# Layer norm's channel sums as two fp32r matmuls on high and low parts, and a last token tile that accumulates on top of sums that ScalarE has laid into PSUM

## The chip, the core and the metric

The kernel runs on one core of one Trainium2 chip. TensorE (PE in the profile; PEld is its weight load), VectorE (DVE), ScalarE (ACT), GpSimd (POOL) and SyncE (SP) run their own instruction streams and wait for one another by semaphores. The metric is the device time of one execution in microseconds; the time before is the median of three runs.

## What is computed

One decoder layer on 1024 tokens of 1024 channels in float32: a Conformer convolution branch and a gated linear recurrence are merged, projected and added to the input; a squared-ReLU MLP follows, and a last RMSNorm. The change touches two places: the layer norm in the convolution branch, and the end, where the MLP's result is added to the residual and normalised.

```python
def layer_norm(x, g, b):
    mu = jnp.mean(xf, axis=-1, keepdims=True)
    xc = xf - mu
    y = xc * lax.rsqrt(jnp.mean(xc * xc, axis=-1, keepdims=True) + EPS)
    return y * g + b
...
u = jax.nn.silu(layer_norm(u, ln_g[l], ln_b[l]))       # after the width-31 convolution
y_a = jnp.einsum("bsc,cd->bsd", u, w_a_out[l])
...
f = jnp.square(jax.nn.relu(jnp.einsum("bsd,df->bsf", h, w_1[l])))
x = x + jnp.einsum("bsf,fd->bsd", f, w_2[l])
return rms_norm(x, g_final)
```

## The kernel before

Every large product is made in float32 precision out of fp32r matmuls. An operand is split into a high part (a ScalarE `Copy` into an fp32r tile) and a low part (the source minus the high part, by VectorE, or by an accumulating DMA that GpSimd issues), and three matmuls are accumulated: high by high, high by low, low by high. A matmul takes 128x128 weights and 512 columns, one PSUM bank of float32. The stages, in the order of time, are the projections from the input with the convolution and the recurrence, the branch products, the output projection, the MLP's first matrix, and its second.

**Layer norm (span 628 to 763 us).** Channels lie along the partitions and tokens along the free axis, so a mean over channels is a product with a 128x128 matrix of 1/1024 (`onesm`, line 110), which also spreads the result over all partitions. The eight channel tiles of the convolution are added up beforehand by accumulating DMAs into one 128x1024 tile `ysum` (`sum_up`, lines 599 to 608). The layer norm runs beside the product of the other branch, `b_mm(j)` for j = 0 to 7 (line 1107): 72 matmuls each, whose two results are gated by `b_out` (line 1123, VectorE at line 1127). `n_mean` (line 1146) is called within `b_mm(2)` and issues one plain float32 matmul for each half of the tokens into banks `mu0` and `mu1`; `n_center` (line 1152) subtracts the mean from the eight pieces of each half (VectorE), squares them (ScalarE) and adds the squares up into `vacc[o]` (VectorE); `n_var` (line 1174), at the start of step j = 4, issues one float32 matmul for each half; `n_root` and `n_scale` (lines 1180 and 1189) make the reciprocal root and apply it. In this stage the order of ScalarE, VectorE, TensorE, SP and GpSimd is that of the program text (`manual_schedule(engines=ENGINES)`, line 1632); `later` puts VectorE work into a list that `vector_work` issues. Tiles come from pools: `T` has 37 buffers of 128x1024 (line 37), the pool behind `EV` has 14 of 128x512 (line 1073), `bank` has 8 PSUM banks.

**The end (span 1496 us to the end).** Seven partial results of the second MLP matrix have been summed into `acc` tiles and two PSUM tiles `keep`; `fold(q2)` (line 1929, VectorE) combines them with the residual into `res`, the sums so far of four token tiles. The last group of channels is multiplied directly: `last_mm(t)` (line 1942) takes 24 matmuls for token tile t, 12 for each half of the output columns, in the order t = 0, 1, 4, 5, then 2, 3, 6, 7. Tiles 0 to 6 of the order use the pool of tags `d`; tile 7 uses two tiles of the pool that held `keep`, one for each half, so that its first half can be read while its second half is being multiplied. `finish(t)` (line 1964) adds `res` to each half (VectorE, line 1973), squares with a running sum (ScalarE, line 1974), makes the reciprocal root in small steps, scales by it and by `gfin`, and stores. For t = 7 the scaling by `gfin` is done ahead (line 1979), and the two halves are scaled (lines 1985 and 1987) and stored from two queues. Here the order on the engines is the compiler's scheduler's: it takes the ready instruction of highest priority, and `finish(7)` has its priority raised by 100 places.

Of the kernel before, what the change touches and what calls it, by code (L numbers as in the profile page):

```python
# [10 lines left out]
F32R = mybir.dt.float32r  # L11
I32 = mybir.dt.int32
AF = mybir.ActivationFunctionType
ALU = mybir.AluOpType

P = 128
S = 1024
D = 1024
HS = 512
# [6 lines left out]
EPS = 1e-6  # L26
# [5 lines left out]
def trunk_kernel(ctx: ExitStack, tc: tile.TileContext, x, xt_in, xt_eo, vecs, w_in, w_a_out, w_b_out,  # L32
                 w_rg, w_o, w_1, w_2, g_final, out):

    nc = tc.nc
    cp = ctx.enter_context(tc.tile_pool(name="consts", bufs=1))
# [8 lines left out]
    def T(name, dt=F32, shape=(P, S)):  # L45
        return tp.tile(list(shape), dt, tag="T", name=name)
# [8 lines left out]
    HALVES = (slice(0, HS), slice(HS, S))  # L55
# [53 lines left out]
    make_identity(nc, ident)  # L109
    onesm = cp.tile([P, P], F32, name="onesm")  # L110
    nc.gpsimd.memset(onesm, 1.0 / D)
    ones = cp.tile([P, P], F32, name="ones")
    nc.gpsimd.memset(ones, 1.0)

# [307 lines left out]
    MM = 0.227  # L422
    TAP = 0.67

    def at(e, cost, ready=0.0):
        clk[e] = max(clk[e], ready) + cost
        return clk[e] + 0.1
# [152 lines left out]
    ysum = []  # L580
# [18 lines left out]
    def sum_up(now, most=8):  # L599

        while summed and summed[0][0] <= now and most:
            most -= 1
            j = summed.pop(0)[1]
            if not ysum:
                ysum.append(T("ysum"))
                nc.gpsimd.dma_start(ysum[0], yd[j])
            else:
                nc.gpsimd.dma_start(ysum[0], yd[j], accum_op=ALU.add)
# [91 lines left out]
    todo, fresh = [], []  # L700

    def later(ready, cost, f, *a):

        todo.append((ready, len(todo), cost, f, a))
# [87 lines left out]
    for i in range(2, NZ):  # L792
        n = zseq.index((i, 1))
# [19 lines left out]
    with tc.manual_schedule(engines=ENGINES):  # L813
        for s in range(3, NC1):
# [49 lines left out]
            for d in range(6):  # L864
                if s - d in EXP:
# [10 lines left out]
                    t = 3 * g + d - 2 - lag  # L876
# [27 lines left out]
    vp = stage.enter_context(tc.tile_pool(name="evac", bufs=7, reuse_waits="tile"))  # L904
# [168 lines left out]
    vp = early.enter_context(tc.tile_pool(name="evac3", bufs=14, reuse_waits="tile"))  # L1073
# [6 lines left out]
    def bank(name):  # L1080
        return zp.tile([P, HS], F32, tag="z", name=name)

    def low(l, src, h):
        tt(l, src, h.bitcast(F32), ALU.subtract)  # L1084
# [58 lines left out]
    def n_pieces(o):  # L1143
        return [(kk, c2, i) for kk in range(2) for c2 in range(2) for i in range(2)]

    def n_mean():
        for o in range(2):
            mean[o] = bank(f"mu{o}")
            nc.tensor.matmul(mean[o], onesm, ysum[0][:, HALVES[o]], start=True, stop=True)
            at("P", 4 * MM)  # L1150

    def n_center(o):
        held = []
# [18 lines left out]
        dve(0.63, held[0][0], add, held[0][1])  # L1172

    def n_var(o):
        pv = bank(f"var{o}")
        nc.tensor.matmul(pv, onesm, vacc[o], start=True, stop=True)
        at("P", 4 * MM)
        rstd[o] = pv

    def n_root(o):  # L1180
        pv = rstd[o]
# [450 lines left out]
    with tc.manual_schedule(engines=ENGINES):  # L1632
        for j in range(8):
            clk["A"], clk["V"] = max(clk["A"], clk["P"] + 0.5), max(clk["V"], clk["P"] - 2)
            if j == 0:
                b_load(1)
                b_gate(0)
            if j == 4:
                n_var(0)
                n_var(1)  # L1640
            if j:
                b_out(j - 1)
            b_gate(j + 1) if j < 7 else None
            b_mm(j)
            if j < 7:
                b_parts(j + 1)
            if j < 6:
                b_load(j + 2)
            vector_work(clk["V"])
            if j < 2:  # L1650
                sum_up(clk["P"])
                vector_work(math.inf if j else clk["P"] - 0.3)
                if j:
                    n_load()
                    sum_up(math.inf)
            elif j < 4:
                n_center(j - 2)
            elif j == 4:
                n_root(0)
                n_root(1)  # L1660
            elif j == 5:
                for b in (0, 1, 3, 2):
                    n_scale(b % 2, b // 2)
            elif j == 6:
                g_parts("a", 1, 0)
                g_parts("a", 1, 1)
                g_load("a", 0, 0)
                g_load("a", 1, 0)
            else:
                g_load("a", 2, 0)  # L1670
                g_get(0, g_lhs)
                g_load("a", 3, 0)
                g_get(1, g_lhs)
                g_t("a", 0, 1, 2)
                g_t("a", 1, 1, 2)
                g_parts("a", 2, 0)
                g_get(2, g_lhs)
                g_parts("a", 2, 1)
                g_load("a", 0, 1)
                g_get(3, g_lhs)  # L1680
                g_load("a", 1, 1)
            vector_work(clk["V"])
        b_out(7)
        for n in range(len(gseq) + 1):
            clk["A"], clk["V"] = max(clk["A"], clk["P"] + 0.5), max(clk["V"], clk["P"] - 2)
            g_get(n - 1, g_post)
            if n in (o0 + 22, u0 + 2):
                x1_root(int(n > u0))
            if n > o0:
                vector_work(clk["V"])  # L1690
                if n == u0:
                    to_mlp()
            g_get(n + 3, g_gate)
            g_get(n, g_mm)
            g_get(n + 4, g_lhs)
            g_get(n + 5, g_sums)
            for f, *a in GX.get(n, ()):
                f(*a)
            vector_work(clk["P"] - 0.3)
# [239 lines left out]
        tt(a[5], a[5], x22[q2], ALU.add)  # L1939
        return (a[2], a[3]), (a[4], a[5])  # L1940

    def last_mm(t):
        r0 = t // 4
        c0 = t % 4 * P
        if t < 7:
            ps = pd.tile([P, S], F32, tag="d", name=f"e{t}", bufs=2)
            outs = [ps[:, h] for h in HALVES]
        else:
            outs = [pk.tile([P, S], F32, tag="k", name=f"e{t}{c}", bufs=2)[:, 0:HS] for c in range(2)]
        for c, o in enumerate(outs):  # L1950
            todo, late = [], []
            for kk in range(2):
                ah, al = (v3(a) for a in last["a", 10 * (r0 + 1) + kk + 1])
                b_h, b_l = (v3(a) for a in last["b", 10 * (kk + 1) + c + 1])
                for k in range(KC):
                    w, wl = ah[:, k, c0:c0 + P], al[:, k, c0:c0 + P]
                    todo += [(w, b_h[:, k, :]), (wl, b_h[:, k, :])]
                    late += [(w, b_l[:, k, :])]
            todo += late
            for n, (a, b) in enumerate(todo):  # L1960
                nc.tensor.matmul(o, a, b, start=n == 0, stop=n == len(todo) - 1)  # L1961
        return outs

    def finish(t, pss, res):
        o = T(f"out{t}")
        y = T(f"y_{t}")
        rows = out.rearrange("(n o) d -> o n d", o=2)[t // 4, (t % 4) * P:(t % 4 + 1) * P, :]
        st = cp.tile([P, 6], F32, tag="stl", name=f"st_last{t}", bufs=2)
        sa, sb, v, s, u, r = (st[:, i:i + 1] for i in range(6))
        lo, hi = HALVES  # L1970
        for hf, a in ((0, sa), (1, sb)):
            h = HALVES[hf]
            tt(y[:, h], res[hf][:, HALVES[t % 2]], pss[hf], ALU.add)
            nc.scalar.activation(o[:, h], y[:, h], AF.Square, accum_out=a)
            if t == 7 and hf == 0:
                nc.vector.tensor_scalar(sa, sa, 1.0 / D, EPS, ALU.mult, ALU.add)
        if t == 7:
            for h in HALVES:
                tt(y[:, h], y[:, h], gfin[:, h], ALU.mult)
            nc.vector.scalar_tensor_tensor(v, sb, 1.0 / D, sa, ALU.mult, ALU.add)  # L1980
            nc.scalar.activation(s, v, AF.Sqrt)
            nc.vector.reciprocal(r, s)
            nc.vector.scalar_tensor_tensor(u, r, v, r, ALU.mult, ALU.mult)
            nc.vector.tensor_scalar(u, u, -0.5, 1.5, ALU.mult, ALU.add)
            nc.vector.tensor_scalar(o[:, lo], y[:, lo], r, u, ALU.mult, ALU.mult)
            nc.sync.dma_start(rows[:, lo], o[:, lo])
            nc.vector.tensor_scalar(o[:, hi], y[:, hi], r, u, ALU.mult, ALU.mult)
            nc.scalar.dma_start(rows[:, hi], o[:, hi])
        else:
            tt(v, sa, sb, ALU.add)  # L1990
            nc.vector.tensor_scalar(v, v, 1.0 / D, EPS, ALU.mult, ALU.add)
            newton_rstd(r, v, s, u)
            nc.vector.scalar_tensor_tensor(o, y, r, gfin, ALU.mult, ALU.mult)
            nc.sync.dma_start(rows, o)

    for q2 in range(2):
        res = fold(q2)
        for t in (2 * q2, 2 * q2 + 1, 4 + 2 * q2, 5 + 2 * q2):
            pss = last_mm(t)
            with tc.high_priority(100 if t == 7 else 0):  # L2000
                finish(t, pss, res[t // 4])

# [83 lines left out]
```

## Time and profile before

| | |
|---|---|
| median of 3 runs | 1550.47 us (1550.38 to 1551.23) |
| the profiled execution, own time | 1550.73 us |
| its span, first to last instruction | 1548.9 us |
| outside the span | 1.83 us |
| granted TensorE clock, mean | 0.998 |
| matmuls | 6804, busy 1537.6 us |
| VectorE, ScalarE, GpSimd busy | 1213.1, 900.4, 189.0 us |

In the rows of a timeline the first number is the start in us from the span's start, the second the time from the start of the first to the end of the last instruction of the row, then the engine, the line, the operation with its output and inputs, the shape and the count; square brackets give idle time of the engine ahead of it and what ended it. Rows of one engine overlap by some hundredths of a microsecond, and matmuls by more, because they are pipelined: what a matmul costs is read from start to start. `sq` is the name in the profile for the tile `vacc[o]` as well, `e` for the last tiles, `st_last` for the small columns of `finish`.

### The profile page before, as it was taken

What the parts mean: (1) busy time and instruction counts of PE and PEld (TensorE: products, weight loads), DVE (VectorE), ACT (ScalarE), POOL (GpSimd) and SP (SyncE); (2) the same over time, 40 slices, a digit from 0 to 9 for tenths busy, and PEclk for the clock granted to TensorE, in tenths of its full rate; (3) what the DMA queues carried; (4) which work ended last, traced back from release to release, by engine and by line L of the source; (5) the groups of instructions that cost most, each with busy time, mean ns of one, the idle gap of its engine ahead of it and who ended that gap; (6) DMA issues with size and microseconds to landing.
All of it is one profiled execution on the core that took longest, in us unless ns stands there. A gap on an engine that the chain in (4) does not pass through costs nothing. (4 is left out here: it accounts for less than half of the span.)

```text
span 1548.9 us, 19074 instructions
## 1 busy us (share of the span) xinstructions
PE 1537.6 (99%) x6804; PEld 1264.6 (82%) x6804; DVE 1213.1 (78%) x1640; ACT 900.4 (58%) x1260; POOL 189.0 (12%) x226
## 2 busy tenths in 40 slices
PE   9999999999999999999999999999999999999997
PEld 7878888788888888878888888888888888888886
DVE  6999989999899983468568869765555558888897
ACT  6748677576667667435275777445444475555552
POOL 0000000002222222000022322000000011111110
PEclk9999999999999999999999999999999999999999
DMA  8653654678999789854579878523333779888852
GB/s 347 169 127 93 162 138 135 156 229 215 263 265 258 194 209 258 275 187 121 184 199 302 197 168 207 207 75 131 114 118 109 238 214 235 225 222 221 197 123 109
DMA packets 124943, 294.18 MB, mean 190 GB/s; under 512 B 12464, under 2 KB 30512, under 8 KB 124848
## 3 DMA queue, kind: packets, MB, share of 16 engines
q1 hardware_dynamic: 93312, 213.00, 40.5%
q0 software_dynamic: 31392, 79.71, 28.1%
q8 instruction: 53, 0.87, 0.2%
q14 instruction: 42, 0.34, 0.1%
q10 hardware_dynamic: 144, 0.26, 0.1%
HBM read 152.93 MB, written 58.72 MB: 137 GB/s over the span
## 5 line engine op out<-in xcount | busy, mean ns | idle before, releaser
L734 PE MATMUL z<-xh,win_h 128*128 128x512 f32 x400 | 124.8, 390 | 0.0
L734 PE MATMUL z<-xl,win_h 128*128 128x512 f32 x400 | 123.4, 389 | 0.0
L1858 DVE TENSOR_TENSOR acc<-acc,d 128x1024 f32<-128x1024 f32 x72 | 87.8, 1219 | 33.4 <-PE d L1846 32.7
L734 PE MATMUL z<-xh,win_l 128*128 128x512 f32 x400 | 99.4, 391 | 0.0
L734 PEld LDWEIGHTS z<-xh,win_l 128*128 128x128 f32 x400 | 75.1, 188 | 16.9
L734 PEld LDWEIGHTS z<-xh,win_h 128*128 128x128 f32 x400 | 75.0, 188 | 16.6 <-ACT win_h L68 0.4
L647 DVE SCALAR_TENSOR_TENSOR y<-u,vec,y 128x511 f32<-128x511 f32 (+14 forms) x120 | 88.3, 736 | 0.0
L734 PEld LDWEIGHTS z<-xl,win_h 128*128 128x128 f32 x400 | 75.1, 188 | 15.8
L647 DVE SCALAR_TENSOR_TENSOR yt<-u,vec,yt 128x511 f32<-128x511 f32 (+6 forms) x112 | 82.5, 736 | 0.0
L647 DVE SCALAR_TENSOR_TENSOR y<-yt,csum,y 128x511 f32<-128x511 f32 (+6 forms) x112 | 82.4, 736 | 0.0
L541 ACT ACTIVATE g<-rg,vec 96x1024 f32<-96x1024 f32 x32 | 35.6, 1114 | 79.6 <-PE rg L531 79.5
L1526 ACT ACTIVATE o<-s 128x512 fp32r<-128x512 f32 x58 | 34.7, 623 | 52.8 <-DVE s L1511 31.3
L67 POOL DMA_DIRECT2D win_l<-win_raw x25 | 21.7, 867 | 319.6 <-ACT win_l L66 259.6
L475 DVE SCALAR_TENSOR_TENSOR v<-xb,vec,v 128x1023 f32<-128x1023 f32 (+2 forms) x36 | 46.2, 1282 | 11.4 <-ACT v L466 10.4
L67 POOL DMA_DIRECT2D zo<-zw x42 | 36.3, 864 | 134.0 <-ACT zo L66 120.6
L1120 PE MATMUL yb<-hgh,wb_h 128*128 128x512 f32 x168 | 52.6, 394 | 0.0
L1120 PE MATMUL yb<-hgl,wb_h 128*128 128x512 f32 x168 | 51.8, 389 | 0.0
L66 ACT ACTIVATE zo<-zw 128x512 fp32r<-128x512 f32 x42 | 26.3, 626 | 30.4 <-DMA zw<-in_w_in_dram 8.4
L67 POOL DMA_DIRECT2D db_1l<-wr x7 | 6.0, 862 | 309.7 <-DMA wr<-in_w_dram 254.0
L1120 PE MATMUL yb<-hgh,wb_l 128*128 128x512 f32 x168 | 41.0, 389 | 0.0
L1084 DVE TENSOR_TENSOR o<-s,o 128x512 fp32r<-128x512 f32 x58 | 38.8, 683 | 0.0
L1120 PEld LDWEIGHTS yb<-hgh,wb_h 128*128 128x128 f32 x168 | 31.6, 188 | 7.4 <-issue 1.0
(1783 smaller groups left out, 4666.7 us busy)
## 6 DMA issues: line engine op xcount, KB each, us to landing
w_raw<-in_w_dram SPq DMA_DIRECT2D x36, 512.0 KB, 5.6
fr<-fd SPq DMA_DIRECT2D x32, 512.0 KB, 5.8
wr<-in_w_dram SPq DMA_DIRECT2D x32, 512.0 KB, 6.5
zw<-in_w_in_dram SPq DMA_DIRECT2D x28, 512.0 KB, 5.8
win_raw<-in_w_in_dram SPq DMA_DIRECT2D x25, 512.0 KB, 4.2
win_l<-win_raw POOLq DMA_DIRECT2D x25, 512.0 KB, 4.5
zo<-zw POOLq DMA_DIRECT2D x42, 256.0 KB, 5.4
gates<-zg SPq DMA_DIRECT2D x32, 256.0 KB, 3.8
```

The costliest lines, as they stand in the source:

```text
L66: nc.scalar.activation(l, src, AF.Copy, scale=-1.0)
L67: nc.gpsimd.dma_start(l, src, accum_op=ALU.add)
L475: nc.vector.scalar_tensor_tensor(v[:, d:S], a[:, 0:S - d], cbw_c[:, w * 12 + t:w * 12 + t + 1], v[:, d:S], ALU.mult, ALU.add)
L541: nc.scalar.activation(a, gps.pop((n, gi))[:HD, :], AF.Sigmoid, bias=(ba_c, bx_c)[gi][:, n:n + 1])
L647: nc.vector.scalar_tensor_tensor(o[:, k:], a[:, 0:HS - k], c, o[:, k:], ALU.mult, add)
L734: nc.tensor.matmul(zps[s][:, HALVES[hf]], w[:, k, :], xw[k][part][hf], start=n == 0, stop=n == 23)
L1084: tt(l, src, h.bitcast(F32), ALU.subtract)
L1120: nc.tensor.matmul(ps[hf], a, b[:, HALVES[hf]], start=n == 0, stop=n == len(todo) - 1)
L1526: nc.scalar.activation(o[:, 0], src, AF.Copy)
L1858: tt(acc[p, q2], acc[p, q2], ps, ALU.add)
```

## The change

1. A constant `onesr` (1/1024 as fp32r, 128x128) is made once by ScalarE.
2. `ysum` is split into two 128x1024 tiles from pool `T`: high by ScalarE, low by VectorE. This new function `n_parts` is called at the end of step j = 1.
3. `n_mean` multiplies each half with two fp32r matmuls (high, then low) instead of one float32 matmul.
4. `n_var` splits `vacc[o]` into two 128x512 tiles from the pool behind `EV` (ScalarE, then VectorE), and multiplies in the same way.
5. For token tile 7, ScalarE copies `res` into the two PSUM tiles ahead of the matmuls, which then accumulate on top. `finish(7)` has no addition any more: ScalarE squares straight from PSUM, and VectorE multiplies PSUM by `gfin` into `y`.

```diff
+    onesr = cp.tile([P, P], F32R, name="onesr")
...
+    def n_sum(name, h, l):
+        ps = bank(name)
+        nc.tensor.matmul(ps, onesr, h, start=True, stop=False)
+        nc.tensor.matmul(ps, onesr, l, start=False, stop=True)
+        at("P", 2 * MM)
+        return ps
+
+    def n_parts():
+        nc.scalar.activation(onesr, onesm, AF.Copy)
+        at("A", 0.3)
+        for n in "hl":
+            ysum.append(T(f"ysum{n}", F32R))
+        nc.scalar.activation(ysum[1], ysum[0], AF.Copy)
+        later(at("A", 1.0), 1.2, low, ysum[2], ysum[0], ysum[1])
+
     def n_mean():
         for o in range(2):
-            mean[o] = bank(f"mu{o}")
-            nc.tensor.matmul(mean[o], onesm, ysum[0][:, HALVES[o]], start=True, stop=True)
-            at("P", 4 * MM)
+            mean[o] = n_sum(f"mu{o}", *(a[:, HALVES[o]] for a in ysum[1:]))
...
     def n_var(o):
-        pv = bank(f"var{o}")
-        nc.tensor.matmul(pv, onesm, vacc[o], start=True, stop=True)
-        at("P", 4 * MM)
-        rstd[o] = pv
+        h, l = (vp.tile([P, HS], F32R, tag="ev", name=f"va{n}{o}") for n in "hl")
+        nc.scalar.activation(h, vacc[o], AF.Copy)
+        low(l, vacc[o], h)
+        rstd[o] = n_sum(f"var{o}", h, l)
...
                 if j:
                     n_load()
                     sum_up(math.inf)
+                    n_parts()
...
-    def last_mm(t):
+    def last_mm(t, res):
...
+            for o, a in zip(outs, res[r0]):
+                nc.scalar.activation(o, a[:, HALVES[t % 2]], AF.Copy)
...
-                nc.tensor.matmul(o, a, b, start=n == 0, stop=n == len(todo) - 1)
+                nc.tensor.matmul(o, a, b, start=n == 0 and t < 7, stop=n == len(todo) - 1,
+                                 skip_group_check=t == 7)
...
         for hf, a in ((0, sa), (1, sb)):
             h = HALVES[hf]
+            if t == 7:
+                nc.scalar.activation(o[:, h], pss[hf], AF.Square, accum_out=a)
+                tt(y[:, h], pss[hf], gfin[:, h], ALU.mult)
+                if hf == 0:
+                    nc.vector.tensor_scalar(sa, sa, 1.0 / D, EPS, ALU.mult, ALU.add)
+                continue
             tt(y[:, h], res[hf][:, HALVES[t % 2]], pss[hf], ALU.add)
             nc.scalar.activation(o[:, h], y[:, h], AF.Square, accum_out=a)
-            if t == 7 and hf == 0:
-                nc.vector.tensor_scalar(sa, sa, 1.0 / D, EPS, ALU.mult, ALU.add)
         if t == 7:
-            for h in HALVES:
-                tt(y[:, h], y[:, h], gfin[:, h], ALU.mult)
             nc.vector.scalar_tensor_tensor(v, sb, 1.0 / D, sa, ALU.mult, ALU.add)
```

More of the change, by code (lines that the diff above doesn't have):

```diff
@@ L1998, in trunk_kernel @@
         for t in (2 * q2, 2 * q2 + 1, 4 + 2 * q2, 5 + 2 * q2):
-            pss = last_mm(t)
+            pss = last_mm(t, res)
             with tc.high_priority(100 if t == 7 else 0):
```

## The prediction, made before the changed kernel was run

> **What bounds the kernel now.** First the page's shares of the engines, then the busy time by stretches of the span, then TensorE's list of waits.
>
> ```profile
> PE 1537.6 (99%) x6804; PEld 1264.6 (82%) x6804; DVE 1213.1 (78%) x1640; ACT 900.4 (58%) x1260; POOL 189.0 (12%) x226
> ```
> ```profile
> 628.00:700.00 72.00, 72.00 (x312) 58.22 (x311) 39.84 (x55) 23.94 (x34) 0.00 (x0) 1.00 0.64 216
> 700.00:760.00 60.00, 60.00 (x267) 49.69 (x266) 37.74 (x46) 24.63 (x34) 0.00 (x0) 1.00 0.41 128
> 1540.00:1548.90 8.90, 0.00 (x0) 0.00 (x0) 3.43 (x9) 0.93 (x3) 0.00 (x0) 0.69 0.32 119
> ```
> ```profile
> PE spare L344 <- POOL ones L113: 1.6, 1, 1.6
> PE gu4a L1283 <- ACT u_late L1337: 0.5, 1, 0.5
> ```
>
> TensorE is busy for 99% of the span. The first two stretches hold the layer norm: in 132 us TensorE is busy for 132 us (the second figure), VectorE for 77.6 and ScalarE for 48.6. So a microsecond of TensorE's work removed there is a microsecond of the end, and work given to VectorE and ScalarE is free while TensorE doesn't wait for it. The last stretch is the other kind: TensorE is done, and a chain of short instructions sets the time. The change touches one thing of each kind.
>
> After its start (`spare`) TensorE waits once, at `gu4a`. Saved time would be lost there if the work it waits for didn't itself go back to TensorE.
>
> ```profile
> 932.43 5.36 DVE L452 SCALAR_TENSOR_TENSOR x<-x,vec,rbm 128x512 f32<-128x512 f32 x8 [1.21 <-PE rbm L1452]
> 939.97 2.36 DVE L452 TENSOR_TENSOR gt2u<-x,x 128x1024 f32<-128x1024 f32 x2
> 943.47 1.05 ACT L1225 ACTIVATE gu6h<-gt2u 128x1024 fp32r<-128x1024 f32 x1
> 958.08 0.58 ACT L1337 ACTIVATE u_late<-gu4a 128x512 f32<-128x512 f32 x1
> ```
>
> It does: VectorE starts at 932.43 on TensorE's `rbm` and then works through to `gt2u`, ScalarE splits that at 943.47 and works nearly without a break to 958.08. All of it moves forward with TensorE.
>
> **The sums over channels.** I take TensorE's starts at the boundaries of the 72-matmul blocks from its timeline.
>
> ```profile
> 661.24 0.62 PE L1120 MATMUL yb<-hgh,wb_h 128*128 128x512 f32 x2
> ...
> 668.50 1.88 PE L1149 MATMUL mu<-ysum,onesm 128*128 128x512 f32 x4
> ```
> ```profile
> 679.33 0.62 PE L1120 MATMUL yb<-hgh,wb_h 128*128 128x512 f32 x2
> ```
> ```profile
> 695.66 1.88 PE L1176 MATMUL var<-sq,onesm 128*128 128x512 f32 x4
> ```
> ```profile
> 713.75 0.61 PE L1120 MATMUL yb<-hgh,wb_h 128*128 128x512 f32 x2
> ```
>
> Block 3 alone lasts from 679.33 to 695.66: 16.33 us, or 0.227 for each of 72 fp32r matmuls. Block 2 with the two means in it lasts 679.33 - 661.24 = 18.09 us, and the two variances with block 4 last 713.75 - 695.66 = 18.09 us. Each pair of float32 sums so costs 1.76 us. Afterwards a pair is four fp32r matmuls of the very form of block 3, 4 x 0.227 = 0.91 us. Each pair gives back 0.85 us, both **1.70 us**.
>
> The Trainium skill (FP8 and Floating Point Precision, TensorE Precision Notes) counts a float32 product as four passes through the array. By that a pair would cost 8 x 0.227 = 1.81 us and the change would give 1.81 us here; the two starts, 18.09 and 16.33, say a little less, and the sum keeps 1.70.
>
> What is added lies beside TensorE's work. For the means:
>
> ```profile
> 594.95 1.22 POOL L608 DMA_DIRECT2D ysum<-yd  x1
> ...
> 656.00 0.85 ACT L1098 ACTIVATE wb_h<-wb_raw 128x768 fp32r<-128x768 f32 x1 [3.22 <-PE yb L1120]
> ...
> 661.21 1.29 DVE L1127 TENSOR_TENSOR sb<-yb,sb 128x512 f32<-128x512 f32 x2 [11.25 <-PE yb L1120]
> ```
>
> The last addition into `ysum` is issued at 594.95, over 50 us ahead. In ScalarE's order the copies `onesr` and `ysumh` come before the row at 656.00, ahead of which it idles 3.22 us; the copy of 128x1024 costs about 1.05 (the `gu6h` row has the form), the small one less. VectorE's low part, about 1.2 by its `gt2u` row (2.36 for two of that size), falls into 11.25 idle microseconds ahead of 661.21. TensorE needs both at 668.50: over 7 us to spare. TensorE has a new wait there, with the rest of block 2 queued behind it; every microsecond of lateness would be paid in full.
>
> For the variances:
>
> ```profile
> 691.00 1.57 ACT L1098 ACTIVATE wb_h<-wb_raw 128x768 fp32r<-128x768 f32 x2
> 691.13 0.69 DVE L1156 TENSOR_TENSOR sq<-sq,sq 128x512 f32<-128x512 f32 x1 [0.16 <-ACT sq L1167]
> ```
>
> The last addition of squares ends at 691.82. Behind it come one ScalarE copy (under 0.8, the cost of one of the larger two at 691.00; the other half's has already run) and one VectorE subtraction (0.69): 693.3 at the latest. TensorE arrives at 695.66 - 0.85 = 694.8, so 1.5 us are left. Queued behind the new copies on ScalarE are the two copies at 691.00, which start up to 1.6 us later; their tiles belong to block 5, which starts at 713.75. This is the thinner cover. Were it gone, block 4 and all behind it would wait.
>
> No DMA is added. Two more tiles of 37, and four of 14, are taken for some microseconds. Who could wait for a buffer is SP with the gates' loads and what is queued behind them:
>
> ```profile
> 686.20 1.77 SPq L1105 DMA_DIRECT2D sb<-gates  x2
> 697.81 1.20 SPq L1091 DMA_DIRECT2D wb_raw<-in_w_b_out_dram  x2
> ```
>
> The gates' load that may be pushed out is the one at 686.20, until the variances have been multiplied at the latest (about 696); the next on SP goes at 697.81 as it is. I take nothing for it.
>
> **The last token tile.** The first two rows are the end of tile 6's matmuls and its first addition; the others are the chain behind TensorE's last matmul.
>
> ```profile
> 1534.00 0.62 PE L1961 MATMUL e<-lb22l,la22h 128*128 128x512 f32 x2
> ...
> 1534.66 1.28 DVE L1973 TENSOR_TENSOR y<-acc,e 128x512 f32<-128x512 f32 x2
> ...
> 1539.22 0.61 PE L1961 MATMUL e<-lb22l,la22h 128*128 128x512 f32 x2
> 1539.85 0.68 DVE L1979 TENSOR_TENSOR y<-y,gfin 128x512 f32<-128x512 f32 x1
> 1540.45 0.68 DVE L1973 TENSOR_TENSOR y<-acc,e 128x512 f32<-128x512 f32 x1
> 1541.16 0.63 ACT L1974 ACTIVATE out<-y 128x512 f32<-128x512 f32 x1 [2.51 <-DVE y L1973]
> 1541.70 0.19 ACT L1974 ACTIVATION_READ_ACCUMULATOR out<-y 128x1 f32 x1
> 1541.92 0.69 DVE L1979 TENSOR_TENSOR y<-y,gfin 128x512 f32<-128x512 f32 x1 [0.79 <-ACT out L1974]
> 1542.53 0.15 DVE L1980 SCALAR_TENSOR_TENSOR st_last<-st_last 128x1 f32<-128x1 f32 x1
> ```
>
> TensorE ends at 1539.83; call it E. The addition starts at E + 0.62, since VectorE is still scaling the first half; the square at E + 1.33; the scaling by `gfin` at E + 2.09, since it overwrites what the square reads; the step that joins the sums at E + 2.70. From there on nothing changes.
>
> Afterwards the square starts as soon as TensorE ends. What the trace doesn't show directly is a square from PSUM with a running sum beside a VectorE read of the same bank in this place, but an earlier stage has just that pair:
>
> ```profile
> 922.84 0.60 ACT L1414 ACTIVATE sq<-tr 128x512 f32<-128x512 f32 x1 [0.48 <-PE tr L1409]
> 923.34 0.19 ACT L1414 ACTIVATION_READ_ACCUMULATOR sq<-tr 128x1 f32 x1
> 923.57 4.87 DVE L1418 COPY x1r<-tr 128x512 f32<-128x512 f32 x8 [3.19 <-ACT sq L1414]
> ```
>
> VectorE had been idle for 3.19 us, TensorE's tile was ready for both, and it waited until ScalarE had read the bank and given out its sum: 0.73 us after the square's start. I take the same order here, because the square stands first in the program. VectorE's wait for TensorE is 0.04 us (tile 6: 1534.66, after matmuls that end at 1534.00 + 0.62). So: square at E + 0.04, product with `gfin` at E + 0.77, and, a step of 0.61 later (1541.92 to 1542.53), the join at E + 1.38. That is **1.32 us** earlier than E + 2.70. The bounds: with no waiting of VectorE at all, the join needs only the square's sum, E + 0.77 and a gain of 1.93; with VectorE held up by tile 6 up to one scaling longer, a gain of 0.1.
>
> Is VectorE free at E + 0.77?
>
> ```profile
> 1537.19 0.20 ACT L98 ACTIVATE st_last<-st_last 128x1 f32<-128x1 f32 x1 [0.42 <-DVE st_last L1991]
> ...
> 1538.58 1.29 DVE L1993 SCALAR_TENSOR_TENSOR out<-y,st_last,gfin 128x1024 f32<-128x1024 f32 x1
> ```
>
> Tile 6's final scaling runs from 1538.58 to 1539.87. If tile 7's first square takes ScalarE ahead of tile 6's root (1537.19), and its first product then takes VectorE, the scaling moves back by some 0.7 us, to end near 1540.55; the product is due at E + 0.77 = 1540.60. Just free.
>
> The copies of `res` into PSUM are new (ScalarE, SBUF to PSUM, a form that this trace lacks). The nearest rows are 0.58 (from PSUM, `u_late`) and 0.63 (within SBUF, line 1974); I take 0.6 each. What counts is when they can run:
>
> ```profile
> 1519.60 1.22 DVE L1937 TENSOR_TENSOR acc<-acc,acc 128x1024 f32<-128x1024 f32 x1
> 1522.20 1.22 DVE L1939 TENSOR_TENSOR acc<-acc,xb 128x1024 f32<-128x1024 f32 x1
> 1525.95 0.63 ACT L1974 ACTIVATE out<-y 128x512 f32<-128x512 f32 x1 [3.43 <-DVE st_last L105]
> ```
>
> The sums are complete at 1520.8 and 1523.4, ScalarE idles 3.43 us ahead of 1525.95, and tile 7's 24 matmuls of 0.227 begin at about E - 5.4 = 1534.4. Ten microseconds of cover, if the scheduler takes them when they are ready, as it does with `fold`'s own additions, which the program has behind tile 5 and VectorE ran between earlier tiles. They cost nothing then.
>
> **Sum.** 1.70 + 1.32 = 3.02 us. The profiled execution would go from 1550.73 to 1547.71, its span from 1548.9 to 1545.9. It lies 0.26 above the median of the three runs, and from that median the forecast is 1550.47 - 3.02 = **1547.45 us**.
>
> **The rivals.**
>
> *The two reads of a bank go side by side.* Then the join comes at E + 0.77 and 0.61 more is gained: 1546.84. Only the shape of the new code speaks for it; the row at 923.57 speaks against it. The Trainium skill (PSUM — Partial Sum Buffer, PSUM bank collisions raise a hardware error) says of ScalarE and VectorE reads too that they must not meet in a bank and have to be guarded by semaphores; the wait of 3.19 us agrees. Chance 0.05.
>
> *Tile 6 is in the way.* If its final scaling starts just ahead of tile 7's second product, VectorE is up to 1.2 us late (1.29 less overlap): 1547.45 + 1.2 = 1548.65 at the most. For it: the margin above is 0.05 us. Against it: tile 6's steps are all ready earlier, and the priority favours tile 7. Chance 0.08.
>
> *ScalarE copies `res` too late: slower than before.* If the copies queue where the program has them, behind tile 6's squares and its root, the first starts at about 1537.4 and ends at 1538.0, where tile 7 would have begun at 1534.4: TensorE waits 3.6 us, 0.6 more than all that is gained, which gives 1551.05. It decides from the point where the first copy starts after 1533.8; the gain is gone when it starts after about 1536.8. For it: the copies stand behind `finish(6)` in the program and have no raised priority. Against it: their inputs are ready ten microseconds earlier, and ScalarE is idle. Chance 0.06.
>
> *The layer norm's gain is lost on the way* to a wait that is not TensorE's own, at `gu4a` or in a load that comes later because its buffer does. Then 1.32 remain: 1549.15. For it: VectorE is busy for 78% of the span, so some stage may stand near its limit. Against it: the one wait listed and its origin in TensorE. Chance 0.06. *Buffers or the scheduler's order change more than that*, with waits beyond what is saved, over 1553.6: chance 0.03.
>
> **How the numbers follow.** The forecast has 0.72. A change of 0.2%, 3.1 us, is about what a measurement of this kernel can tell from none, and the forecast lies at that very bound (1547.37): half of its chance falls on either side, as the scatter of the runs (0.85 us between three) and the few hundredths in the terms decide. Faster by over 0.2%: 0.36 + 0.05, and 0.05 of the two middle rivals, whose terms can turn out smaller, 0.46. Slower by over 0.2%: 0.03. Between: 0.51. The forecast with its terms' bounds is 1546.9 to 1548.0; the range takes in the side-by-side reads and most of tile 6's case and leaves out the late copies and what lies beyond: 1546.6 to 1548.8.
>
> **What would show it.** From block 2's start to block 3's 17.24 us instead of 18.09, and the same for the variances; no wait of TensorE at `mu` or `var`; the copies of `res` in ScalarE's row near 1520 to 1525; the square 0.04 after TensorE's last matmul; the product with `gfin` 0.73 after the square's start and waiting for ScalarE; 1.38 us from TensorE's end to the join, and from there 6.4 us to the span's end as before (1548.9 - 1542.53). A new gap in TensorE's row between 690 and 700 us or after 1533, or a longer wait at `gu4a`, would make the prediction wrong.

## The result, and the profile after

The changed kernel takes 1548.58 us, the median of 22 runs; the kernel before 1551.45 us, also of 22, the first three of which are the runs of the table above. The ratio is 0.9983, with a 95% interval of 0.9976 to 0.9989: **0.17% faster**. The forecast was 1547.45 us. Of the 1.13 us between, 0.98 is the starting point (1551.45 instead of the 1550.47 of three runs); the change itself was forecast at 3.02 us and came out, between the medians, at 2.87.

| | before | after |
|---|---|---|
| profiled execution, own time | 1550.73 us | 1549.04 us |
| its span | 1548.9 us | 1547.2 us |
| TensorE busy | 1537.6 us | 1535.6 us |
| granted TensorE clock, mean | 0.998 | 0.998 |

First, from TensorE's timeline of the kernel after, the layer norm: the start of block 2, matmuls of the means, the start of block 3, the first matmul of the variances, the start of block 5.

```profile
661.46 0.61 PE L1121 MATMUL yb<-hgh,wb_h 128*128 128x512 f32 x2
...
668.72 0.39 PE L1149 MATMUL mu<-ysumh,onesr 128*128 128x512 f32 x1
668.96 0.40 PE L1150 MATMUL mu<-ysuml,onesr 128*128 128x512 f32 x1
...
669.42 0.39 PE L1150 MATMUL mu<-ysuml,onesr 128*128 128x512 f32 x1
...
678.72 0.62 PE L1121 MATMUL yb<-hgh,wb_h 128*128 128x512 f32 x2
...
695.04 0.40 PE L1149 MATMUL var<-vah,onesr 128*128 128x512 f32 x1
...
712.29 0.62 PE L1121 MATMUL yb<-hgh,wb_h 128*128 128x512 f32 x2
```

Block 2 lasts 678.72 - 661.46 = 17.26 us and the variances with block 4 last 712.29 - 695.04 = 17.25, each instead of 18.09: 1.67 us given back. The matmuls of a sum start 0.23 to 0.24 us apart, as fp32r matmuls do in block 3, and no bracket shows idle time ahead of them.

Now the end, from the timeline of all engines: TensorE's last matmuls, tile 6's final scaling, and the chain behind the last matmul.

```profile
1537.83 1.29 DVE L2013 SCALAR_TENSOR_TENSOR out<-y,st_last,gfin 128x1024 f32<-128x1024 f32 x1
1539.00 0.62 PE L1978 MATMUL e<-lb22l,la22h 128*128 128x512 f32 x2
1539.03 0.68 DVE L1993 TENSOR_TENSOR y<-e,gfin 128x512 f32<-128x512 f32 x1
1539.63 0.14 DVE L1995 TENSOR_SCALAR st_last<-st_last 128x1 f32<-128x1 f32 x1
1539.65 0.60 ACT L1992 ACTIVATE out<-e 128x512 f32<-128x512 f32 x1 [1.97 <-PE e L1978]
1540.15 0.19 ACT L1992 ACTIVATION_READ_ACCUMULATOR out<-e 128x1 f32 x1
1540.37 0.69 DVE L1993 TENSOR_TENSOR y<-e,gfin 128x512 f32<-128x512 f32 x1 [0.60 <-ACT out L1992]
1540.98 0.15 DVE L2000 SCALAR_TENSOR_TENSOR st_last<-st_last 128x1 f32<-128x1 f32 x1
```

TensorE ends at E = 1539.62. The square starts at E + 0.03; the product with `gfin` is held by ScalarE (the bracket) until 0.72 after the square's start; the join is at E + 1.36 instead of E + 2.70. That is 1.34 us.

But E itself moved by only 0.21 us, from 1539.83 to 1539.62. TensorE's list of waits after shows the larger part of the reason.

```profile
PE gu4a L1297 <- ACT u_late L1351: 1.6, 1, 1.6
PE z L258 <- ACT xh L227: 0.5, 1, 0.5
PE z4e L933 <- DMA zo<-zs: 0.2, 1, 0.2
PE z L258 <- DVE xl L231: 0.2, 1, 0.2
```

The wait at `gu4a` has grown from 0.5 to 1.6 us, and three short waits in the first stages are new. The balance of the two spans: block 2 starts 0.22 later (first stages), the sums give 1.67, between block 5 and E 1.25 is lost, 1.1 of it at `gu4a`, the end gives 1.34, and the stores behind the join take 6.22 instead of 6.37. Together 0.22 - 1.67 + 1.25 - 1.34 - 0.15 = -1.69 us, the -1.7 of the spans. So in this pair of executions the gain of the sums seems to be lost at `gu4a`, while the medians of many runs show nearly all of it. Which of the two holds had to be tried.

### The profile page after: what moved, and what is told of

It reads as the page before. It is cut to its first block, busy times and chain, and to the rows that moved or that the text cites. A ratio compares the mean times of both kernels' runs of the same rounds, so it can differ in the third digit from the quotient of the medians.

```text
span 1547.2 us, 19086 instructions
## 1 busy us (share of the span) xinstructions
PE 1535.6 (99%) x6804; PEld 1264.6 (82%) x6804; DVE 1214.5 (78%) x1641; ACT 903.6 (58%) x1266; POOL 188.6 (12%) x226
```

## The experiments

The theories. **A:** `gu4a` hangs on a load that lands when it lands; a TensorE that comes 1.67 us earlier waits that much longer there, and the gain of the sums is lost. **B:** the landing of that load scatters from execution to execution, whatever the kernel, so the wait at `gu4a` does too; on the mean the gain passes through. The load can be seen in both kernels, in the timelines of ScalarE and VectorE. Before:

```profile
939.97 2.36 DVE L452 TENSOR_TENSOR gt2u<-x,x 128x1024 f32<-128x1024 f32 x2
942.41 0.63 ACT L66 ACTIVATE gu<-w_raw 128x512 fp32r<-128x512 f32 x1 [3.82 <-DMA w_raw<-in_w_dram]
943.47 1.05 ACT L1225 ACTIVATE gu6h<-gt2u 128x1024 fp32r<-128x1024 f32 x1
```

After:

```profile
938.51 2.35 DVE L453 TENSOR_TENSOR gt2u<-x,x 128x1024 f32<-128x1024 f32 x2
942.07 0.63 ACT L66 ACTIVATE gu<-w_raw 128x512 fp32r<-128x512 f32 x1 [4.91 <-DMA w_raw<-in_w_dram]
943.12 1.04 ACT L1239 ACTIVATE gu6h<-gt2u 128x1024 fp32r<-128x1024 f32 x1
```

VectorE comes 1.46 us earlier to `gt2u`, as TensorE does, but ScalarE, which takes a piece of weights from `w_raw` ahead of `gu6h`, waits for its load until 942.07 instead of 942.41. The gain stops at that row.

**One part alone: the layer norm.** The kernel before with the changed sums; `last_mm` and `finish` as they were.

```diff
-    def last_mm(t, res):
+    def last_mm(t):
...
-            for o, a in zip(outs, res[r0]):
-                nc.scalar.activation(o, a[:, HALVES[t % 2]], AF.Copy)
```

> The fp32r sums alone; the last token tile as before. Both theories: blocks 2 and 4 with their sums take 17.25 us (18.09 before), 1.7 us less of TensorE. Theory A (the load of w_10 lands at a time that the busy DMA engines set, so TensorE's lead is lost at gu4a): the wait of TensorE's weight loads at gu4a is about 2.0 us as in the changed kernel (0.9 before), and the kernel is only 0.5 to 0.8 us faster than before. Theory B (that wait scatters from one execution to the next, whatever the kernel): it lies anywhere between 0.5 and 2.5, and the kernel is about 1.7 us faster on average.

Measured: 1549.26 us, ratio 0.9990 (0.9981 to 0.9999). Blocks of 17.26 and 17.25 us; wait at `gu4a` 0.7 us; join at E + 2.70. The wait is short although the sums are the new ones. The time alone leaves both theories standing: by its interval it is 0.2 to 2.9 us less than before.

**One part alone: the last tile.** The sums are plain float32 again.

```diff
-            mean[o] = n_sum(f"mu{o}", *(a[:, HALVES[o]] for a in ysum[1:]))
+            mean[o] = bank(f"mu{o}")
+            nc.tensor.matmul(mean[o], onesm, ysum[0][:, HALVES[o]], start=True, stop=True)
...
+        nc.tensor.matmul(pv, onesm, vacc[o], start=True, stop=True)
```

> The last token tile alone; layer norm as before. Both theories: from TensorE's last matmul to the step that joins the sums 1.37 us (2.70 before), copies of res near 1520 to 1525, 1.3 us faster than before. Theory A: the wait at gu4a is 0.9 us as before. Theory B: anywhere between 0.5 and 2.5.

Measured: 1550.49 us, ratio 0.9994 (0.9985 to 1.0004); blocks of 18.10 and 18.09 us, join at E + 1.37. The two parts alone give 0.10 and 0.06%, together the 0.17% of the whole within their intervals; the second by itself can't be told from none. In TensorE's list of waits of this kernel, whose sums are the old ones, stands

```profile
PE gu4a L1283 <- ACT u_late L1337: 1.2, 1, 1.2
```

more than twice the 0.5 us of the kernel before, whose program is the same up to the last tile. Theory A has no room for that.

**The load one step earlier.** In the changed kernel, the load that ScalarE waited for changes places with one that VectorE needs.

```diff
-        0: ((x1_rows, 4, 5, 6, 7),), 1: ((up_load, 4, (0,)), (up_load, 0, (1,))),
-        2: ((x1_diag, 1), (x1_spread, 1), (up_load, 5, (0,)), (up_load, 1, (1,))),
+        0: ((x1_rows, 4, 5, 6, 7),), 1: ((up_load, 4, (0,)), (up_load, 5, (0,))),
+        2: ((x1_diag, 1), (x1_spread, 1), (up_load, 0, (1,)), (up_load, 1, (1,))),
```

> The changed kernel with the load of w_10 put ahead of the second halves' loads of tiles 0 and 1 on SP, so that it is the second of four instead of the third. Both theories take the load for what ScalarE waits for at 942.07: it lands 1 to 2 us earlier, ScalarE's split there waits no longer for it, and the wait at gu4a falls to about 0.9 us, 1.1 less than in the changed kernel, whose time it should beat by about 1 us (theory A) or by the mean excess of the wait, 0 to 1 us (theory B). If VectorE's gt2u or the displaced loads bound it as well, the wait stays above 1.5.

Measured: 1547.88 us, ratio 0.9975 (0.9966 to 0.9985). The same rows of its timeline:

```profile
937.85 0.63 ACT L66 ACTIVATE gu<-w_raw 128x512 fp32r<-128x512 f32 x1 [1.38 <-DMA w_raw<-in_w_dram]
937.87 2.35 DVE L453 TENSOR_TENSOR gt2u<-x,x 128x1024 f32<-128x1024 f32 x2
...
939.12 1.06 ACT L1239 ACTIVATE gu6h<-gt2u 128x1024 fp32r<-128x1024 f32 x1
940.64 0.69 DVE L1524 TENSOR_TENSOR s<-w_raw 128x512 f32<-128x512 f32 x1 [0.42 <-DMA w_raw<-in_w_dram]
```

`gu6h` no longer waits for the load, and TensorE's wait at `gu4a` is 0.2 us. Now VectorE waits for the load that was put back, at 940.64. The row shows the way from the load to the wait; it can't show what a typical execution pays.

**The join ahead of the last product.** In the changed kernel, the product of the second half with `gfin` stands behind the join and the root.

```diff
-                tt(y[:, h], pss[hf], gfin[:, h], ALU.mult)
                 if hf == 0:
+                    tt(y[:, h], pss[hf], gfin[:, h], ALU.mult)
...
+            tt(y[:, hi], pss[1], gfin[:, hi], ALU.mult)
```

> The changed kernel with the last product by gfin put behind the step that joins the sums and behind ScalarE's root. If VectorE may not read the bank beside ScalarE (as predicted), the join starts 0.73 us after the square's start, 0.61 earlier than in the changed kernel, and the reciprocal waits for the product: the end comes 0.3 us earlier. If VectorE may read beside ScalarE, nothing changes at the join. At gu4a it repeats the changed kernel: theory A about 2.0 us of wait, theory B anywhere between 0.5 and 2.5.

Measured: 1547.77 us, ratio 0.9979 (0.9970 to 0.9987). From its timeline, with E = 1538.19:

```profile
1538.23 0.60 ACT L1992 ACTIVATE out<-e 128x512 f32<-128x512 f32 x1 [1.97 <-PE e L1978]
...
1538.95 0.16 DVE L2000 SCALAR_TENSOR_TENSOR st_last<-st_last 128x1 f32<-128x1 f32 x1 [0.60 <-ACT out L1992]
1539.02 0.68 DVE L2002 TENSOR_TENSOR y<-e,gfin 128x512 f32<-128x512 f32 x1
1539.14 0.20 ACT L2001 ACTIVATE st_last<-st_last 128x1 f32<-128x1 f32 x1 [0.23 <-DVE st_last L2000]
1539.62 0.15 DVE L2003 RECIPROCAL st_last<-st_last 128x1 f32<-128x1 f32 x1
...
1541.29 0.37 ACTq L2009 DMA_DIRECT2D out_dram<-out  x1
```

The join comes at E + 0.76, and that is the whole 0.6 us of the product; but VectorE starts the product at once, while ScalarE takes the root, and the reciprocal waits for its end at 1539.62. The last store is issued at E + 3.10 instead of E + 3.46: 0.36 us remain. In TensorE's waits this kernel, the same as the changed one up to its last instructions, has

```profile
PE gu4a L1297 <- ACT u_late L1351: 0.3, 1, 0.3
```

against 1.6: with the same program up to there, the wait differs by 1.3 us between two executions.

**Both of the last two edits together,** on two chips:

> The changed kernel with two further edits: in the stage of the gated recurrence the load of the next weight piece goes out one step earlier, and in the last token tile the second product with gfin stands behind the join and the root, so that it no longer delays the join. Each alone gave: the earlier load a wait of 0.7 us at gu4a, the later product a join at E + 0.76 and the last store's issue at E + 3.10 instead of E + 3.46. If the two are independent (they lie 600 us apart), both are seen together: wait 0.7 or less, join at E + 0.76, last issue at E + 3.10, a span of 1544.9 to 1545.3 us, a median some 0.3 us below that of the earlier load alone, about 1547.5. If the end's gain is swallowed by the landing of the last stores, the span is no shorter than the earlier load's 1545.2.

> The changed kernel with the earlier load and the later last product once more, beside the changed kernel itself on the same chip: 0.3 us less from the end (last issue at E + 3.10 instead of E + 3.46), and 0 to 1 us less from the wait at gu4a.

Measured: 1547.46 us, ratio 0.9969 (0.9957 to 0.9981), and 1547.52 us, ratio 0.9973 (0.9963 to 0.9984). The changed kernel on the same chips gave 1548.64 and 1548.82 (below). So 1.2 and 1.3 us less by the medians, though the intervals of the ratios overlap: it is the fastest version here, and how much of that is real beyond the 0.36 us at the end isn't settled. Join and last issue are as expected, in the second run at E + 0.76 and E + 3.10 (1539.03 and 1541.37 after 1538.27); the wait at `gu4a` is 0.8 us in both, not the 0.2 seen with the earlier load alone. In the first, the span of 1547.8 us misses what was expected: block 2 started at 663.20, 1.25 to 2.73 us later than in every other execution but one, after waits for transfers in the first stages.

**The earlier load in the kernel before.**

> The kernel before with the earlier load alone, its sums plain float32 and its last tile unchanged: blocks of 18.09 us, join at E + 2.70. Theory B (the load's landing scatters in each execution, and with it TensorE's wait at gu4a): wait about 0.7 us, no load named ahead of the high parts of gu, and a time lower than before by the mean excess of that wait, 0.2 to 0.8 us. Theory A (the landing is held by the transfers ahead and costs only a kernel whose TensorE comes earlier): no gain, since this kernel's TensorE comes late; the same time as before within 0.15 us.

Measured: 1550.68 us, ratio 0.9996 (0.9987 to 1.0005). TensorE has no wait at `gu4a` in its list any more, and still the time can't be told from that of the kernel before. By the interval it lies between 2.0 us less and 0.8 us more, so this run doesn't choose between the two expectations; a load that is worth some tenths in the mean fits it.

**The changed kernel twice more,** unaltered:

> The changed kernel once more, as a further sample of its wait at gu4a beside the others. Theory A: the wait is again 1.6 to 2.0 us. Theory B: anywhere between 0.7 and 2.0 us, with the span changing by as much; the blocks stay at 17.25 us, the join at E + 1.37, and the ratio to the kernel before at 0.998.

> The changed kernel, for the comparison on one chip: a ratio to the kernel before of 0.998, and a third sample of its wait at gu4a (2.0 and 0.9 us so far, by the weight load's row).

Measured: 1548.64 us, ratio 0.9978 (0.9969 to 0.9987), and 1548.82 us, 0.9981 (0.9972 to 0.9990). From the lists of waits, one line each:

```profile
PE gu4a L1297 <- ACT u_late L1351: 0.5, 1, 0.5
```
```profile
PE gu4a L1297 <- ACT u_late L1351: 0.7, 1, 0.7
```

**Theory A falls, B stands.** All the profiled executions with the load in its old place, by their lists of waits: with the new sums 1.6, 0.7, 0.3, 0.5, 0.6, 1.0, 0.9 and 0.7 us (mean 0.79), with the old sums 0.5 and 1.2 (mean 0.85). The load also moves with TensorE: with the new sums `gt2u` starts at 938.08 in the mean and ScalarE's piece of weights at 940.90, with the old ones at 940.33 and 943.16, so both come some 2.2 us earlier. From `gt2u` to that piece the single executions show 2.33 to 3.56 us; where this scatter comes from was not traced, and with the old sums there are only two samples. The profile after, taken alone, happened to be the one with the longest wait.

**The copies of `res` made late.** The changed kernel, but the copies carry a bias of zero times a number of tile 6, so that they must wait for it. The first run takes that number from tile 6's second sum of squares (its edit is shown), the second from its first addition, the third from its first sum of squares:

```diff
-                nc.scalar.activation(o, a[:, HALVES[t % 2]], AF.Copy)
+                nc.scalar.activation(o, a[:, HALVES[t % 2]], AF.Identity, bias=none[0])
...
+            if t == 6:
+                none.append(cp.tile([P, 1], F32, name="none"))
+                nc.vector.tensor_scalar(none[0], sb, 0.0, None, ALU.mult)
```

> The changed kernel, but the copies of res into PSUM take a bias of 0 times tile 6's sum of squares, so that they can't run before tile 6 has been squared; what is computed is the same. It prices the rival of the late copies. By the prediction's rule, the first copy starts near E6 + 2.6, about 1536.6 us, instead of 1520.4, and TensorE waits there for some 3.2 us: nearly all of the 3.0 us that the two parts give, so a time within 0.5 us of the kernel before. If TensorE had slack there, the time would stay that of the changed kernel.

> As the run with the late copies, but their bias is 0 times a column of tile 6's first sum, so that they wait for tile 6's first addition only; what is computed is the same. The first copy then starts some 1.4 us earlier than in that run, and TensorE waits about 1.7 us instead of 3.2. There the wait was followed by a granted clock of 0.50 for some 6.7 us, which cost 2.9 us more than the wait. Theory C (the clock drops after a wait of any length above a microsecond): 1.7 + 2.9, a span some 4.6 us longer. Theory D (it drops only after a longer wait; the 1.6 us at gu4a left it at 1.00): the clock stays at 1.00 and the cost is the wait alone, so about 1.7 us above the changed kernel, near 1550.3.

> The same with the first half's sum of squares as the source of the bias, so that the copies wait for tile 6's first square, between the two others: a wait of about 2.6 us. Theory C: 2.6 + 2.9 us. Theory D gives 2.6 alone if 2.6 us is short enough; if the drop comes from windows of time that do not start with the wait, some executions have it and others not, and their times lie in two groups some 2.9 us apart.

Measured: 1553.05, 1552.54 and 1552.77 us, ratios 1.0007 (0.9998 to 1.0016), 1.0005 (0.9996 to 1.0014) and 1.0005 (0.9996 to 1.0014). Against the changed kernel of the same chip that is 4.4, 3.7 and 3.95 us by the medians. The first fence is the first run's timeline; the second its busy time by stretches, where the last three figures are the granted clock, the share of the DMA engines and GB/s:

```profile
1534.64 1.30 ACT L1966 ACTIVATE e<-acc,none 128x512 f32<-128x512 f32 x2 [0.29 <-DVE none L2019]
...
1535.38 0.80 PE L1978 MATMUL e<-lb11h,la21h 128*128 128x512 f32 x1 [3.19 <-ACT e L1966]
...
1536.40 0.63 PE L1978 MATMUL e<-lb11h,la21h 128*128 128x512 f32 x1
1536.82 0.63 PE L1978 MATMUL e<-lb11h,la21l 128*128 128x512 f32 x1
```
```profile
1535.30:1538.00 2.70, 2.62 (x6) 2.16 (x7) 1.77 (x5) 0.76 (x3) 0.00 (x0) 0.50 0.00 0
1538.00:1541.00 3.00, 3.00 (x8) 2.35 (x8) 0.22 (x1) 0.04 (x1) 0.00 (x0) 0.50 0.45 178
```

TensorE idles for 3.19 us, and then its matmuls start 0.42 us apart instead of 0.23: the granted clock is 0.50. In finer stretches the clock drops at 1534.62, while TensorE is still idle and 2.4 us after tile 6's last matmul (its end is at 1532.19), and comes back at 1541.44. From its first matmul to its last one's end tile 7 takes 1543.94 - 1535.38 = 8.56 us; in the profile after it took 1539.62 - 1534.01 = 5.61. So 2.95 us come on top of the wait.

The other two runs were to shorten the wait to 1.7 and 2.6 us. They didn't: in both, ScalarE runs the copies behind tile 6's two squares, and TensorE's wait is 2.78 us. Theories C and D are therefore not told apart at 1.7 us. In the second run the clock was 0.50 again, from 1534.84 (2.1 us after TensorE's last matmul) to 1541.66, and tile 7 took 1544.08 - 1535.49 = 8.59 us. In the third the half clock came later; from its stretches:

```profile
1536.00:1537.00 1.00, 0.69 (x3) 0.60 (x4) 0.06 (x1) 0.99 (x3) 0.00 (x0) 1.00 0.02 8
1537.00:1538.00 1.00, 1.00 (x6) 0.77 (x5) 0.83 (x5) 0.00 (x0) 0.00 (x0) 0.81 0.00 0
1538.00:1539.00 1.00, 1.00 (x4) 0.81 (x3) 1.00 (x1) 0.00 (x0) 0.00 (x0) 0.50 0.00 0
```

TensorE starts again at 1536.31, runs at the full clock for over a microsecond, and only then is halved, from 1537.63 to 1541.04; tile 7 takes 1543.69 - 1536.31 = 7.38 us.

Wait and longer tile together are 6.14, 5.76 and 4.55 us in the three profiles, more than the medians differ by; how often and for how long the other executions had the half clock was not traced. The ten times of the third run, 1550.82 to 1554.93 us, don't fall into the two groups that its expectation thought possible.

## Why the prediction was right, and where it was wrong

**The step that failed** is in how the numbers follow: "A change of 0.2%, 3.1 us, is about what a measurement of this kernel can tell from none", with most of the chance (0.51) put on "between". The gain of 0.17% is under that bound to the letter, yet it is told from none clearly: over 22 runs each, the ratio's interval is 0.9976 to 0.9989, some 0.07% to either side, and two further comparisons gave 0.9978 and 0.9981 with 1 outside their intervals too. No row of the prediction stands behind the bound; the one scatter that it quotes, 0.85 us between three runs, is 0.05%. So the bound was three times too wide, and it stood just at the size of a gain whose terms were both known to some hundredths. With the terms as they were, a gain of 0.19% that the runs tell from none should have had by far the most.

**The starting point** was the other miss. Three runs gave 1550.47 us and 22 gave 1551.45, so the measured 1548.58 came near the upper end of the range (1548.8) although both terms were right to 0.03 us.

**The sums over channels: right.** 1.70 us forecast, 1.67 found (18.09 to 17.26 and 17.25). The new work is hidden as said; the rows of ScalarE and VectorE after:

```profile
649.10 0.29 ACT L1155 ACTIVATE onesr<-onesm 128x128 fp32r<-128x128 f32 x1
649.30 1.04 ACT L1159 ACTIVATE ysumh<-ysum 128x1024 fp32r<-128x1024 f32 x1
650.38 1.22 DVE L1085 TENSOR_TENSOR ysuml<-ysum,ysumh 128x1024 fp32r<-128x1024 f32 x1 [0.19 <-ACT ysumh L1159]
```
```profile
690.42 0.61 ACT L1190 ACTIVATE vah<-sq 128x512 fp32r<-128x512 f32 x1
691.15 1.47 DVE L1085 TENSOR_TENSOR val<-sq,vah 128x512 fp32r<-128x512 f32 x2
691.27 0.63 ACT L1190 ACTIVATE vah<-sq 128x512 fp32r<-128x512 f32 x1 [0.24 <-DVE sq L1170]
691.81 1.56 ACT L1099 ACTIVATE wb_h<-wb_raw 128x768 fp32r<-128x768 f32 x2
```

The low part of the means is done at 651.60, 17 us ahead of TensorE; that of the variances at 692.62, 2.4 ahead of 695.04. What queued behind on ScalarE (`wb_h`) moved by 0.8 us and delayed nothing.

**The end: right.** 1.32 us forecast, 1.34 found, by the steps as they were put: the square at E + 0.03, the product held by ScalarE until 0.72 after it, the join at E + 1.36. The rule taken from an earlier stage, that VectorE waits until ScalarE has read the bank and given out its sum, held here and, at 0.72 us each time, in the last tile alone and in both repeats of the changed kernel.

**Tile 6: right that it is out of the way, wrong on why.** Its scaling was to be pushed back to end near 1540.55, with 0.05 us to spare. It runs from 1537.83 to 1539.12, since ScalarE takes tile 6's root before tile 7's first square, and VectorE no longer has tile 7's first addition between tile 6's small steps. The first row is from the kernel before, the other two are from the kernel after:

```profile
1537.15 0.69 DVE L1973 TENSOR_TENSOR y<-acc,e 128x512 f32<-128x512 f32 x1
```
```profile
1536.75 0.20 ACT L98 ACTIVATE st_last<-st_last 128x1 f32<-128x1 f32 x1 [0.42 <-DVE st_last L2011]
...
1536.99 0.60 ACT L1992 ACTIVATE out<-e 128x512 f32<-128x512 f32 x1
```

VectorE is idle for 0.60 us ahead of the last product. The margin is over half a microsecond, and it was not the reasoning of the prediction that gave it.

**The copies: right in place, wrong in price.** They run at

```profile
1520.41 0.60 ACT L1966 ACTIVATE e<-acc 128x512 f32<-128x512 f32 x1 [0.31 <-DVE acc L1952]
...
1523.00 0.60 ACT L1966 ACTIVATE e<-acc 128x512 f32<-128x512 f32 x1 [0.93 <-DVE acc L1954]
```

in the window 1520 to 1525 and at the 0.6 us that were taken. Had they been late, though, the loss would have been more than the wait that the rival counted: with 3.19 us of wait, tile 7 took 2.95 us longer as well, because the clock was halved.

**"All of it moves forward with TensorE": right on the mean, not in each execution.** The prediction followed `gu4a` back to VectorE's chain and so to `rbm`, and did not quote the row at 942.41, where ScalarE waits 3.82 us for a load just ahead of `gu6h`. That row says the wait has a second origin, and that the profile after could turn out a microsecond off either way; it did. By the prediction's own sign, "a longer wait at `gu4a`", that profile spoke against it; the two repeats of the changed kernel, with waits of 0.5 and 0.7 us, have spans of 1545.8 us, against the 1545.9 that were forecast. That this fits to 0.1 us is in part luck, since the start of block 2 alone scatters by more. The rival that the layer norm's gain is lost there describes that one profile, and the waits of the other runs refute it as the rule.

## What to carry to other kernels

Work taken off an engine that was busy for 99% of the span came back in its stage nearly as forecast (1.67 us for 1.70); it had been sized from start-to-start times of the same instruction form in the trace. Whether the total shows it is a question of how many runs stand behind the median, so take the bound of "no change" from the interval that the comparison will have, not from the spread of a few runs. And where a wait of the bounding engine has a load in its chain, compare that stage over several executions before you explain a difference with it: here the changed kernel, unaltered, waited 0.5, 0.7 and 1.6 us.

## What the runs showed of the hardware that was not expected

- A wait of TensorE of 2.78 to 3.19 us went with a granted clock of 0.50, for 6.8 us in two runs and 3.4 us in the third, at a cost of 2.95, 2.98 and 1.77 us beyond the wait; the waits of up to 1.6 us at `gu4a` left it at 1.00. Some 2 us without a matmul were enough for the drop to come: 2.4 and 2.1 us in the first two of these runs, and 2.0 us at the end of the changed kernel with the load one step earlier, where the clock fell at 1539.55 after a last matmul that ended at 1537.54. In one run the drop came over a microsecond after the matmuls had resumed. The Trainium skill (TensorE: Matmul & The Clock Gate, Part 1: The HAM clock gate) tells of a half rate after an idle window of about 3.4 us, with windows that run freely. That the drop doesn't begin with the gap agrees with it, and so do the lengths, 3.4 us and twice that; gaps of 2.78 us, though, were enough in both runs that had one, which is less than its figure, and the measurement decides.
- The start of block 2, up to which TensorE's instructions are the same in all of them, lay between 660.47 and 663.20 us in the fourteen profiled executions. In two of them (663.20 and 662.98) the lists of waits name waits for transfers of 0.5 to 1.0 us ahead of it; the spread as a whole was not traced.
- A float32 matmul of 128x512 costs 0.88 us of TensorE where fp32r takes 0.227: (18.09 - 16.33) / 2 against 16.33 / 72, a factor of 3.9.
